# First unit of the mixer in four stages, a shorter way from routing to gather, and expert results merged during the last expert unit

## The chip, the cores and the metric

The kernel runs on one core of a Trainium2 chip. The metric is the device time of one execution in microseconds (us). TensorE (PE) multiplies, VectorE (DVE), ScalarE (ACT) and GpSimd (POOL) do the work between the products, and SyncE (SP) issues most of the DMAs. TensorE has two clock levels, 1.2 and 2.4 GHz.

## What is computed

A backbone of two layers over 256 context tokens and 256 latent tokens, 512 rows of 1024 numbers, all in float32. Each layer is

```python
hl = modulate(rmsnorm(xl, norm1[i]), sh1l, sc1l)       # the same for context, with its own shifts and scales
yc, yl = mixer(hc, hl, ...)                            # layer 0: RG-LRU and gated linear attention; layer 1: attention
xl = xl + g1l * yl
hl2 = modulate(rmsnorm(xl, norm2[i]), sh2l, sc2l)
xl = xl + g2l * hier_moe(hl2, ...)
```

The shifts, scales and gates (`sh`, `sc`, `g`, six rows of 1024 a layer and stream) are products of SiLU of a condition with `w_ada`, the adaLN columns. `hier_moe` takes for each token the best of four groups and in it the best two of four experts, and adds their results with their weights; an expert is `(silu(t @ w1) * (t @ w3)) @ w2`, 1024 to 512 to 1024. Layer 0 computes both streams, layer 1 only the latent one at its end.

## The kernel before

A float32 product is made of three: `whi` x `hhi`, `wlo` x `hhi` and `whi` x `hlo`, where `hi` is a value rounded by an ACT copy and `lo` the rest, a DVE (or POOL) subtraction of 128x1024. A weight tile `raw` is 1 MB (128 partitions x 2048); SP issues them in the order of a list (`plan`, `feed`, `pump`), one when a buffer (slot) comes free. The language's scheduler sets the order of each engine's instructions; each engine then works in that order.

**First unit.** `norm_T` loads the tokens into `xres`, squares them, turns them (transposes on PE into `acc` and `aux`) and scales them by the row factors into `xw`. `first_unit` computes the first 512 columns of the projection `w_in` as four sums (m) over eight blocks of 128 (k), in four steps n of two k each. Step n needs the adaLN columns n: `ad0` (8 matmuls `ad<-raw,cT`), and `ad0_cols`: an ACT copy, four transposes, and DVE's `v`, `A` and `B`. `finish` then applies `A` and `B` to `xw` and splits the result into `hhi` (ACT) and `hlo` (DVE). The list `AD0` says behind which product group each of the nine pieces is written. `LO_U0 = '1111'` puts the `wlo` of this unit on POOL. DVE also makes `lam`, a chain of small steps for the RG-LRU, at the same time.

**Route of layer 0.** After each tile's last products `route` makes logits and `choose` the ranks of groups and experts; the masks `Mb` go to PE, which counts per expert (`aux<-Mb,tri`). For tile 3 (`LATE_T`) the tokens' modulation (`xa`, `h2x`) runs on ACT and POOL. `route_end` with `units`, `weights`, `prepare` and `tables` ranks the experts by load: eight big ones get a unit of 128 rows each (a single unit), eight small ones share four units of 64 + 64 (two-expert units). One-hot matrices `oh` times `vals` give `t0i`, the rows that each unit gathers and scatters, and its weights `t0w`. POOL then clears `xg` and gathers the first two units' tokens from DRAM (`h2d`). The branch at line 1667, for overflow that doesn't occur with these inputs, follows. Copies `raw<-ident` on POOL hold back some weight DMAs.

**Experts of layer 0.** The loop `for e in range(NU)` goes over 12 units in the order `SEQ`; numbers 0 to 7 are single, 8 to 11 two-expert. In unit e `hidden(e, 1, 0)` and `(e, 1, 1)` make the product with w3, `he` multiplies it by the SiLU of the other, PE turns `he`, and ACT (and for a single unit DVE: `hl`) splits it; between these stand the first products of unit e + 1 (`hidden(e + 1, 0, 0)` and `(e + 1, 0, 1)`), then the product with w2. A two-expert unit isn't split; its matmuls are float32 on 64 columns, two records each. The result of unit e goes to DRAM (`yd`) by a scatter on POOL's queue, but for the last two (`N_LAST`), which stay as `yl` and are brought back to tokens by `back` matmuls. `get_parts` reads the scattered results back, two per token tile: `ya` and `yb` (for tiles 0 and 1 both halves of `pt`), in the order 2, 3, 0, 1, on POOL's queue; `add_parts` adds them on POOL, tile 0 on DVE. `finish_moe` adds `back`'s products, multiplies by the gate `row` and adds to `xres`; `norm1` and the `w_qkv` products of layer 1 follow. `LO_KV = "0101"` puts two `wlo` of `w_qkv` on POOL there.

Of the kernel before, what the change touches and what calls it, by code (L numbers as in the profile page):

```python
# [29 lines left out]
SEQ = (0, 8, 1, 2, 9, 3, 4, 10, 5, 6, 11, 7)  # L30
# [15 lines left out]
BEH = 3  # L46
FH = 1
# [11 lines left out]
TICK2 = 0  # L59
# [4 lines left out]
PIN = dict(pair='p', px='g', m0='p')  # L64
AT_SUM = 1
N_SP0 = 2
N_OH = 2
# [7 lines left out]
MID = 0  # L75
# [5 lines left out]
LO_KV = "0101"  # L81
# [9 lines left out]
BH = 1  # L91
AD0 = (1, 3, 3, 4, 5, 5, 8, 8, 8)
U0H = 1
Z_AT = (0, 0, 0, 0, 0, 4, 4, 0)
Z_Q = 0
LO_U0 = '1111'
# [6 lines left out]
AT = 3  # L103
LATE = 0
# [7 lines left out]
LATER = 0  # L112
CAP = 1
X_POOL = ()
F_ORDER = (2, 3, 0, 1)
P_DVE = (0,)
# [35 lines left out]
def backbone(ctx, tc, I, out):  # L152
# [229 lines left out]
    sp.dma_start(mod[0], I["bada"][0])  # L382
# [77 lines left out]
    def ad0_cols(n, sb, v, A1_0, B1_0, bn):  # L460

        act.activation(sb, ad0_ps.pop(n), AF.Copy)
        ps = aux()
        for c in range(4):
            pe.transpose(ps[:, c * P:(c + 1) * P], sb[:, c * P:(c + 1) * P], ident)
        dve.tensor_reduce(v, ps.rearrange("p (c g r) -> p c r g", c=4, g=4)[:, :, 0:2, :], axis=AX.X, op=ALU.add)
        v = v.rearrange("p (s k) i -> p s k i", s=2)
        ks = slice(2 * n, 2 * n + 2)
        nn, bb = (x.unsqueeze(2).to_broadcast([P, 2, 2]) for x in (n1c[:, 0, ks], b1c[:, 0, ks]))
        dve.tensor_tensor(A1_0[:, ks, :], v[:, 1], nn, op=ALU.mult)  # L470
        dve.tensor_tensor(B1_0[:, ks, :], v[:, 0], bb, op=ALU.add)
        dve.tensor_tensor(A1_0[:, ks, :], A1_0[:, ks, :], bn[:, ks, :], op=ALU.add)
# [102 lines left out]
    def unit_cols(name, b, hT, done, tokens_still, tiles=range(4), halves=(0, 1), after=None, on_act=True,  # L575
# [5 lines left out]
        if by_tile:  # L581
# [38 lines left out]
    def norm_T(hp, wide, bd):  # L620
# [3 lines left out]
        A1_0, B1_0, bn = (hp.tile([P, KD, 2], F32, name=n) for n in ("A1_0", "B1_0", "bn"))  # L624
        hhi = hp.tile([P, KD, NTOK], F32R, tag="hhi", name="hhi")
# [32 lines left out]
        for n in range(2):  # L658
            dve.scalar_tensor_tensor(bn[:, :, n:n + 1], b1c[:, 1, :].unsqueeze(2), 1.0, n1c[:, 0, :].unsqueeze(2),
                                     op0=ALU.add, op1=ALU.mult)  # L660

        def finish(n):

            if n == 0:
                scaled(6)
                scaled(7)
            ad0_cols(n, tmp("ad0"), hp.tile([P, 4, 2], F32, tag="v0", name="v0", bufs=2), A1_0, B1_0, bn)
            for k in (2 * n, 2 * n + 1):
# [5 lines left out]
                dve.tensor_tensor(hlo[:, k, :], xt, hhi[:, k, :].bitcast(F32), op=ALU.subtract)  # L674
            if n == 3:
                sp.dma_start(bd, I["bd"])
                sp.dma_start(mod[1], I["bada"][1])
        return (hhi, hlo), finish

    def first_unit(hT, finish, done):  # L680

        hh, hl = hT
        pss = [acc() for _ in range(4)]
        todo = [lambda n=n, f=f: f(n) for n in range(1, 4) for f in (lambda n: ad0(n, 0), lambda n: ad0(n, 1), finish)]
        at = list(AD0)
        ad0(0, 0)
        ad0(0, 1)
        finish(0)
        state["high"] = U0H
        for n in range(4):  # L690
            if n % 2 == 0:
                raw = feed(("w_in", 0, n // 2))
            state["lo"] = pool if LO_U0[n] == "1" else dve
            wh, wl = split(raw[:, n % 2 * 1024:(n % 2 + 1) * 1024])
            state["lo"] = dve
            for m in range(4):
                for kk in range(2):
                    w = [x[:, kk * 512 + m * P:kk * 512 + (m + 1) * P] for x in (wh, wl)]
                    k = 2 * n + kk
                    mm3(pss[m], w, (hh[:, k, :], hl[:, k, :]), k == 0, k == KD - 1)  # L700
                if n == 3:
                    done(m, pss[m])
                while at and at[0] == 4 * n + m:
                    at.pop(0)
                    todo.pop(0)()
        state["high"] = True
# [7 lines left out]
    tid = rt.tile([P, 4], F32, name="tid")  # L714

    def load_router():
# [7 lines left out]
                           base=0, channel_multiplier=-1)  # L724

# [72 lines left out]
    def route(l, NT, tmp, stream, h2_of, router):  # L798
# [12 lines left out]
        R.Mb = rt.tile([P, NT, NE], BF16, tag="Mb", name="Mb")  # L811

        def choose(t):
# [15 lines left out]
            dve.scalar_tensor_tensor(R.Mf[:, t], g0, 0.0, e01, op0=ALU.is_equal, op1=ALU.mult)  # L829
# [43 lines left out]
        def both(t):  # L873
            if MID and t == NT - 2 and not queue:

                queue.extend([lambda: None] * (MID - 1))
                queue.extend((lambda: turn(t, 1), lambda: logits(t, 1, 0), lambda: ends(t)))
                return
# [6 lines left out]
        def tile_(t, on_pool=False):  # L885
# [18 lines left out]
            hv = h2.rearrange("q (k p) -> q p k", k=KD)  # L904
            for n in range(2):
                a = tmp("xa2")
                if on_pool:
                    act.activation(a, x[:, n * 512:(n + 1) * 512], AF.Copy, scale=rss[t])
                    pool.tensor_tensor(a, a, A2[i][n], op=ALU.mult)
                else:  # L910
                    dve.scalar_tensor_tensor(a, x[:, n * 512:(n + 1) * 512], rss[t], A2[i][n], op0=ALU.mult, op1=ALU.mult)
                (pool if on_pool else dve).tensor_tensor(hv[:, n * 64:(n + 1) * 64, :], a.rearrange("q (p k) -> q p k", k=KD),
                    B2[i][n].rearrange("q (p k) -> q p k", k=KD), op=ALU.add)
            sp.dma_start(h2d[l][t * P:(t + 1) * P, :], h2)
# [5 lines left out]
    def route_end(R, l, NT, early=None):  # L920
# [16 lines left out]
        def weights():  # L937

            M = [st(f"M{k}", 4, 4) for k in range(2)]
            ek, tm = (rt.tile([P, 80], F32, tag=n, name=n)[:, 0:NT * NE].rearrange("p (t e) -> p t e", t=NT)  # L940
                      for n in ("ge", "gt"))
            g0 = R.rk[:, :, 0, :].unsqueeze(3).to_broadcast([P, NT, 4, 4])
            mk = [st(f"m{k}", 1) for k in range(2)]
            for k in range(2):
                for t in range(NT):
                    e_ = ek[:, t].rearrange("p (g e) -> p g e", g=4)
                    dve.tensor_scalar(e_, R.rk[:, t, 1:5, :], float(k), None, op0=ALU.is_equal)
                    dve.scalar_tensor_tensor(M[k][:, t], g0[:, t], 0.0, e_, op0=ALU.is_equal, op1=ALU.mult)
            M = [m.rearrange("p t g e -> p t (g e)") for m in M]
            for k in range(2):  # L950
# [1441 lines left out]
```

## Time and profile before

| | us |
|---|---|
| median of 3 runs (lowest, highest) | 1022.91 (1022.48, 1026.24) |
| profiled execution | 1020.54 |
| its span | 1018.8 |
| PE busy in it | 913.9 |
| DVE, ACT, POOL busy | 534.8, 396.2, 162.5 |

The span is the part of the execution between its first and last instruction. Times of rows are us from its start. A row of a timeline is an instruction or several of one form in a row (x3), with start, duration, and in brackets the idle time of the engine just ahead of it and what ended that. Durations of matmuls overlap: the next starts before the last has ended. Stages are cut here at 69 (end of the first unit), 298 (end of the mixer), 335 (first expert product), 565 and 617 (the last two units), 640, 790 and 1011.

### The profile page before, as it was taken

The page shows a single profiled execution, that of the slowest core. Times are in us where ns is not written, and L with a number is a line of the kernel's source. Part 1 is how long each engine was busy: PE and PEld are TensorE (multiplying, and loading weights), DVE is VectorE, ACT ScalarE, POOL GpSimd, SP SyncE. Part 2 cuts the span into 40 slices and gives each one's busy share as a digit, 9 for nine tenths or more (in the row PEclk, how much of TensorE's full clock was granted, in tenths as well). Part 3 has the DMA queues.
Part 4 walks back from the last instruction along what each step waited for, and adds up shares of the span by engine and source line. Part 5 has one row for each costly group of instructions (what it writes and reads, how often), then busy time and mean ns, then how long its engine had stood idle before and what let it go on. Part 6 is the DMA issues. An engine that isn't in the chain of part 4 may idle for free. (4 is left out here: it accounts for less than half of the span.)

```text
span 1018.8 us, 12604 instructions
## 1 busy us (share of the span) xinstructions
PE 913.9 (90%) x4549; PEld 535.3 (53%) x4549; DVE 534.8 (52%) x1039; ACT 396.2 (39%) x687; POOL 162.5 (16%) x163
## 2 busy tenths in 40 slices
PE   5899997999991899989999966998996899999997
PEld 3456465667761555647466433774575444443432
DVE  5458578538587565636456347878657111111112
ACT  3236745144231544637455423453545222121210
POOL 2103332040503400001100233023001000000000
PEclk9899999999995899999999978999998999999999
DMA  9925454559541899999999976845928699999993
GB/s 315 384 100 218 155 198 172 206 182 336 197 160 49 307 419 421 421 420 403 408 422 400 380 306 248 302 171 200 369 95 307 234 419 417 416 418 414 417 414 136
DMA packets 63165, 304.56 MB, mean 299 GB/s; under 512 B 8578, under 2 KB 17666, under 8 KB 35056
## 3 DMA queue, kind: packets, MB, share of 16 engines
q1 hardware_dynamic: 55216, 284.56, 71.4%
q0 software_dynamic: 5120, 14.06, 3.7%
q10 hardware_dynamic: 2752, 4.98, 1.3%
q8 instruction: 40, 0.66, 0.3%
q14 instruction: 37, 0.30, 0.1%
HBM read 294.76 MB, written 12.58 MB: 302 GB/s over the span
## 5 line engine op out<-in xcount | busy, mean ns | idle before, releaser
L144 DVE TENSOR_TENSOR wlo<-raw,whi 128x1024 fp32r<-128x1024 f32 x138 | 170.4, 1250 | 77.4 <-ACT whi L144 70.2
L144 ACT ACTIVATE whi<-raw 128x1024 fp32r<-128x1024 f32 x140 | 146.4, 1057 | 119.4 <-PE acc L144 100.4
L144 PE MATMUL aux<-raw,x 128*64 128x512 f32 x488 | 116.3, 597 | 2.0 <-PEq L2174 1.4
L144 PEld LDWEIGHTS aux<-raw,x 128*64 128x64 f32 x488 | 34.5, 136 | 62.9 <-issue 58.6
L144 PE MATMUL acc<-raw,xf 128*64 128x512 f32 x256 | 62.3, 598 | 2.2 <-DMA raw<-in_w_dram 2.2
L144 PE MATMUL aux<-raw,sl 128*64 128x512 f32 x240 | 58.7, 610 | 0.7 <-ACT sl L144 0.7
L144 PE MATMUL acc<-wlo,xh 128*128 128x512 f32 x128 | 52.1, 407 | 6.4 <-DVE wlo L144 3.6
L144 PE MATMUL ada<-raw,cT 128*32 128x512 f32 x320 | 54.7, 616 | 1.0 <-DMA raw<-in_w_ada_dram 1.0
L144 PE MATMUL acc<-whi,xh 128*128 128x512 f32 x128 | 53.5, 418 | 0.0
L144 PE MATMUL acc<-whi,xl 128*128 128x512 f32 x128 | 51.8, 405 | 0.0
L144 PE MATMUL acc<-raw,hf 128*64 128x512 f32 x128 | 38.6, 659 | 7.9 <-DMA raw<-in_w_dram 7.8
L144 DVE SCALAR_TENSOR_TENSOR aux<-aux,ws,mod 128x512 f32<-128x512 f32 x8 | 6.1, 760 | 73.3 <-PE aux L144 73.3
L144 PE MATMUL acc<-hhi,whi 128*128 128x512 f32 x96 | 38.5, 417 | 6.2 <-ACT hhi L144 6.2
L144 POOL DMA_INDIRECT yd<-y,t0i x10 | 11.7, 1173 | 191.6 <-ACT y L144 156.5
L144 PE MATMUL acc<-whi,h 128*128 128x512 f32 x128 | 41.7, 400 | 0.0
L144 PEld LDWEIGHTS acc<-raw,xf 128*64 128x64 f32 x256 | 19.1, 136 | 38.4 <-issue 30.9
L144 PE MATMUL acc<-hlo,whi 128*128 128x512 f32 x96 | 38.9, 406 | 0.2 <-DVE hlo L144 0.2
L144 PE MATMUL acc<-hhi,wlo 128*128 128x512 f32 x96 | 39.0, 406 | 0.0
L144 DVE TENSOR_TENSOR he<-sl,aux 128x512 f32<-128x512 f32 x8 | 8.4, 1056 | 56.2 <-PE aux L144 56.2
L144 PEld LDWEIGHTS aux<-raw,sl 128*64 128x64 f32 x240 | 18.2, 140 | 37.1 <-issue 35.0
L144 PEld LDWEIGHTS acc<-wlo,xh 128*128 128x128 f32 x128 | 25.1, 196 | 12.3 <-DVE wlo L144 4.0
L144 PEld LDWEIGHTS acc<-whi,xh 128*128 128x128 f32 x128 | 25.0, 195 | 10.1 <-issue 3.5
(444 smaller groups left out, 1850.5 us busy)
## 6 DMA issues: line engine op xcount, KB each, us to landing
raw<-in_w_dram SPq DMA_DIRECT2D x151, 1024.0 KB, 15.0
raw<-in_w_ada_dram SPq DMA_DIRECT2D x38, 1024.0 KB, 6.3
raw<-in_w_dram SPq DMA_DIRECT2D x72, 512.0 KB, 11.5
raw<-in_w_in_dram SPq DMA_DIRECT2D x10, 1024.0 KB, 5.1
raw<-in_w_ada_dram SPq DMA_DIRECT2D x32, 256.0 KB, 6.9
raw<-in_w_qkv_dram SPq DMA_DIRECT2D x6, 1024.0 KB, 12.8
xres<-in_w_dram SPq DMA_DIRECT2D x5, 1024.0 KB
raw<-in_w_out_dram SPq DMA_DIRECT2D x4, 1024.0 KB, 7.5
```

The costliest lines, as they stand in the source:

```text
L144: ins = f(*a, **k)
```

## The change

**First unit.** It is written as four stages. Products of step n come in groups of eight: `whi` x `hhi`, then the adaLN matmuls of n + 1, `whi` x `hlo`, the transposes of these columns, `wlo` x `hhi`. `wlo` is on DVE. The loads of `bada` (512 KB) go behind the unit, `pcol` and the `lam` chain ahead of the norm, `bn` to its start. What may run on which engine's early list (`PIN`) is changed with it.

**Route.** Tile 3's modulation is on DVE, half of its shift behind the choice. `choose` makes the masks `MM` per tile. `to_units` computes only the rows `ix`, with two one-hot steps of 128x512 and 8 matmuls, and the gathers follow at once; `experts` (the order of the weights), `others` (weights, count) and `weights_of` (8 more matmuls) come behind them, then the branch, then the first tokens' transposes and the first weight splits. The first two `xg` lie in one buffer that ACT clears. The copies `raw<-ident` are gone.

**Last units.** `SEQ` ends with 7, 11 in place of 11, 7, so that the last unit is a two-expert one. `get_parts` is written at the start of the last unit but one, `merge` in the last one: DVE adds `ya` and `yb`, multiplies by the gate and adds to `xres`, for tiles 2 and 3 ahead of the unit's second w3 half, for 0 and 1 ahead of its w2. `finish_moe` then only multiplies and adds. `LO_KV` is empty: all `wlo` of `w_qkv` are on DVE.

```diff
-SEQ = (0, 8, 1, 2, 9, 3, 4, 10, 5, 6, 11, 7)
+SEQ = (0, 8, 1, 2, 9, 3, 4, 10, 5, 6, 7, 11)
-PIN = dict(pair='p', px='g', m0='p')
+PIN = dict(pair='p', px='padg', re='da', tb='dag', m0='p', n1='pad', xa='pad')
-LO_KV = "0101"
+LO_KV = ""
-LO_U0 = '1111'
...
     def first_unit(...)
+        for n in range(3):
+            products(n, 0, w)
+            for h in range(2):
+                ad0(n + 1, h)
+            copy, turn, rest = columns(n + 1)
+            copy()
+            x, hi = weights_hi(n + 1)
+            products(n, 1, w)
+            turn()
+            rest()
+            products(n, 2, w)
+            modulate(n + 1)
+            w = hi, weights_lo(x, hi)
+        sp.dma_start(bd, I["bd"])
+        for l in range(2):
+            sp.dma_start(mod[l], I["bada"][l])
...
-    R.finish()
+    R.finish(lambda R: [f() for f in late_h2])
...
-    R.prepare(True)
-    slot_of = R.pk, R.vals
-    ix, wgt = R.tables(0, "t0")
+    ix, weights_of, slot_of = R.to_units()
...
+    for e in range(2):
+        fetch_x(e)
+    R.experts()
...
+    R.others()
+    wgt = weights_of()
...
+    def merge(t):
+        ya, yb = parts[t]
+        dve.tensor_tensor(ya, ya, yb, op=ALU.add)
+        for n in range(2):
+            sl = slice(n * 512, (n + 1) * 512)
+            dve.tensor_tensor(ya[:, sl], ya[:, sl], g2[int(t < 2)][n], op=ALU.mult)
+        dve.tensor_tensor(xres[:, t, :], xres[:, t, :], ya, op=ALU.add)
...
+        if e == NU - N_LAST:
+            get_parts()
...
         hidden(e, 1, 0)
-        get_parts(0, e)
+        if e == NU - 1:
+            for t in F_ORDER[:2]:
+                merge(t)
         hidden(e, 1, 1)
...
+        if e == NU - 1:
+            for t in F_ORDER[2:]:
+                merge(t)
         py = [acc(), acc()]
...
-            y = parts[t][0][:, sl]
-            dve.tensor_tensor(y, ps, y, op=ALU.add)
-            dve.tensor_tensor(y, y, g2[int(t < 2)][n], op=ALU.mult)
-            (pool if (t, n) in X_POOL else dve).tensor_tensor(xres[:, t, sl], xres[:, t, sl], y, op=ALU.add)
+            y = parts[t][1][:, sl]
+            dve.tensor_tensor(y, ps, g2[int(t < 2)][n], op=ALU.mult)
+            dve.tensor_tensor(xres[:, t, sl], xres[:, t, sl], y, op=ALU.add)
```

PE's instructions in the first unit, from the transposes of the first adaLN columns on (`ad`), first before, then after; `hhi`, `hlo` are the tokens, `raw,cT` the adaLN matmuls:

```order
L144 MATMUL aux<-ident,ad_307 128x128 x4
L144 MATMUL ad_343<-raw,cT 32x512 x3
L144 MATMUL acc<-hhi,whi 128x512 x3
L144 MATMUL ad_343<-raw,cT 32x512
L144 MATMUL acc<-hlo,whi 128x512
L144 MATMUL acc<-hhi,wlo 128x512
L144 MATMUL acc<-hhi,whi 128x512
L144 MATMUL acc<-hlo,whi 128x512
L144 MATMUL acc<-hhi,wlo 128x512
L144 MATMUL acc<-hlo,whi 128x512
L144 MATMUL acc<-hhi,wlo 128x512
L144 MATMUL acc<-hhi,whi 128x512
```

```order
L131 MATMUL aux<-ident,ad_301 128x128 x4
L131 MATMUL acc<-hhi,whi 128x512 x8
L131 MATMUL ad_340<-raw,cT 32x512 x8
L131 MATMUL acc<-hlo,whi 128x512 x8
L131 MATMUL aux<-ident,ad_349 128x128 x4
L131 MATMUL acc<-hhi,wlo 128x512 x8
L131 MATMUL acc<-hhi,whi 128x512 x8
L131 MATMUL ad_397<-raw,cT 32x512 x8
L131 MATMUL acc<-hlo,whi 128x512 x8
L131 MATMUL aux<-ident,ad_411 128x128 x4
L131 MATMUL acc<-hhi,wlo 128x512 x8
L131 MATMUL acc<-hhi,whi 128x512 x8
```

The adaLN matmuls of the next step stand together behind the first eight products, and the three kinds of product are no longer mixed one by one.

POOL's instructions from the last row factor (`r`) to the gathers (`xg<-h2d`), before and after; `xa` and `h2x` are the modulation of tile 3:

```order
L144 TENSOR_TENSOR r_2365<-ssq,half_neg 128x1
L144 COPY raw<-ident 128x1
L144 TENSOR_TENSOR xa_2424<-xa_2424,row 128x512
L144 TENSOR_TENSOR h2x<-xa_2424,row 128x64x8
L144 TENSOR_TENSOR xa_2428<-xa_2428,row 128x512
L144 TENSOR_TENSOR h2x<-xa_2428,row 128x64x8
L144 MEMSET xg 128x1024
L144 COPY raw<-ident 128x1
L144 DMA xg<-h2d_112,t0i 128x1024
L144 MEMSET xg 128x1024
L144 DMA xg<-h2d_112,t0i 128x1024
```

```order
L131 TENSOR_TENSOR r_2305<-ssq,half_neg 128x1
L131 TENSOR_TENSOR r_2386<-ssq,half_neg 128x1
L131 DMA xg_2528<-h2d_113,ix 128x1024 x2
L1776 TENSOR_LOAD cnti
L1777 COMPARE_AND_BRANCH
```

Between the last row factor and the gathers nothing is left on POOL.

DVE's instructions at the end of the experts. Before, from the tokens of the last unit (`xl`) to its `hl`; after, from the `he` of the last unit but one over its `hl` to the merge of the third tile (`pt`):

```order
L144 TENSOR_TENSOR xl<-aux,xh 128x512 x2
L144 TENSOR_TENSOR wlo<-raw,whi 128x1024 x2
L144 TENSOR_TENSOR he<-sl,acc 128x128x4
L144 TENSOR_TENSOR wlo<-raw,whi 128x1024 x2
L144 TENSOR_TENSOR pt<-pt 128x1024
L144 TENSOR_TENSOR wlo<-raw,whi 128x1024 x2
L144 SCALAR_TENSOR_TENSOR yl<-acc,t0w,yl 128x512 x2
L144 TENSOR_TENSOR wlo<-raw,whi 128x1024 x3
L144 TENSOR_TENSOR he<-sl,acc 128x128x4
L144 TENSOR_TENSOR wlo<-raw,whi 128x1024
L144 TENSOR_TENSOR hl<-aux,hh 128x512
```

```order
L131 TENSOR_TENSOR he<-sl,acc 128x128x4
L131 TENSOR_TENSOR wlo<-raw,whi 128x1024 x2
L131 TENSOR_TENSOR ya<-ya,yb 128x1024
L131 TENSOR_TENSOR ya<-ya,row 128x512 x2
L131 TENSOR_TENSOR xres<-xres,ya 128x1024
L131 TENSOR_TENSOR ya<-ya,yb 128x1024
L131 TENSOR_TENSOR ya<-ya,row 128x512
L131 TENSOR_TENSOR hl<-aux,hh 128x512
L131 TENSOR_TENSOR ya<-ya,row 128x512
L131 TENSOR_TENSOR pt<-pt 128x1024
L131 TENSOR_TENSOR xres<-xres,ya 128x1024
L131 TENSOR_TENSOR pt<-pt,row 128x512 x2
```

One addition of parts stood among the splits before; now one merge and a half stand ahead of `hl`, and the rest of the four, with the two `yl` of that unit, ahead of the last unit's `he`.

## Rows read from the trace of the kernel before

**Rows 1.** Windows: us, busy PE, PEld, DVE, ACT, POOL, PEclk, DMA share, GB/s.
```profile
0.00:69.00 69.00, 52.57 (x218) 29.20 (x219) 31.88 (x86) 21.12 (x34) 12.12 (x16) 0.95 0.82 285
69.00:298.00 229.00, 219.27 (x1313) 144.51 (x1312) 160.03 (x268) 102.40 (x171) 64.35 (x62) 0.99 0.54 197
298.00:335.00 37.00, 12.79 (x99) 8.34 (x97) 25.25 (x110) 8.34 (x14) 11.61 (x14) 0.61 0.32 111
335.00:565.00 230.00, 220.96 (x974) 136.77 (x972) 128.09 (x142) 126.20 (x155) 27.35 (x26) 0.98 0.99 403
565.00:617.00 52.00, 42.98 (x158) 21.66 (x157) 17.89 (x17) 13.81 (x17) 13.52 (x12) 0.90 0.89 354
617.00:640.00 23.00, 12.21 (x52) 7.02 (x51) 21.62 (x41) 10.50 (x23) 8.76 (x4) 0.71 0.55 212
...
790.00:1011.00 221.00, 216.70 (x1036) 90.86 (x1036) 35.92 (x78) 39.49 (x75) 0.00 (x0) 0.98 0.92 373
```

**Rows 2.** Timeline of PE, first unit: start, us, instruction, idle before and its end.
```profile
27.03 1.65 PE L144 MATMUL acc<-hhi,whi 128*128 128x512 f32 x3 [4.34 <-ACT hhi L144]
...
32.33 0.63 PE L144 MATMUL acc<-hhi,wlo 128*128 128x512 f32 x1
...
36.61 1.06 PE L144 MATMUL ad<-raw,cT 128*32 128x512 f32 x8
...
68.75 0.39 PE L144 MATMUL acc<-hlo,whi 128*128 128x512 f32 x1
68.97 0.39 PE L144 MATMUL acc<-hhi,wlo 128*128 128x512 f32 x1
```

**Rows 3.** Timelines of DVE and POOL, first unit.
```profile
14.14 0.17 DVE L144 TENSOR_SCALAR lam<-lam 128x8 f32<-128x8 f32 x1
...
20.49 4.65 POOL L144 TENSOR_TENSOR wlo<-raw,whi 128x1024 fp32r<-128x1024 f32 x2 [7.30 <-ACT whi L144]
20.60 2.27 DVE L144 TENSOR_SCALAR lam<-lam 128x8 f32<-128x8 f32 x1
...
22.91 2.26 DVE L144 TENSOR_TENSOR lam<-lam,lam 128x8 f32<-128x8 f32 x1
```

**Rows 4.** Timelines of POOL, DVE and PE, route of layer 0.
```profile
306.38 1.32 POOL L144 TENSOR_TENSOR h2x<-xa,row 128x512 f32<-128x512 f32 x1
306.49 1.31 DVE L144 TENSOR_TENSOR gt<-lg 128x80 f32<-128x80 f32 x1
...
316.19 1.22 DVE L144 TENSOR_TENSOR wlo<-raw,whi 128x1024 fp32r<-128x1024 f32 x1
...
323.57 3.70 PE L144 MATMUL aux<-vals,oh 128*128 128x36 f32 x14 [1.12 <-DVE vals L144]
...
328.79 1.25 POOL L144 DMA_INDIRECT xg<-h2d,t0i  x1 [8.31 <-DVE t0i L144]
...
335.16 0.79 PE L144 MATMUL acc<-whi,xh 128*128 128x512 f32 x1
...
343.50 0.70 PE L144 MATMUL acc<-wlo,xh 128*128 128x512 f32 x1 [2.77 <-PEq L1667]
```

**Rows 5.** Timelines of PE, POOL and DVE, last two expert units of layer 0.
```profile
565.22 4.50 PE L144 MATMUL acc<-raw,xf 128*64 128x512 f32 x18
...
576.56 0.60 POOL L144 DMA_DIRECT2D ya<-yd  x1 [7.95 <-DMA yd<-y,t0i]
...
596.00 2.39 POOL L144 TENSOR_TENSOR ya<-ya,yb 128x1024 f32<-128x1024 f32 x1 [4.87 <-DMA yb<-yd]
...
598.83 1.23 DVE L144 TENSOR_TENSOR pt<-pt 128x1024 f32<-128x1024 f32 x1 [19.87 <-DMA pt<-yd]
...
601.24 0.79 PE L144 MATMUL acc<-wlo,xh 128*128 128x512 f32 x1 [3.61 <-DVE wlo L144]
```

**Rows 6.** Timelines of PE and DVE, from the last expert product to layer 1.
```profile
617.18 1.09 PE L144 MATMUL acc<-yl,back 128*128 128x512 f32 x4
...
620.18 1.28 DVE L144 TENSOR_TENSOR pt<-pt,row 128x512 f32<-128x512 f32 x2
...
637.41 2.18 PE L144 MATMUL aux<-ident,pt 128*128 128x128 f32 x9 [4.76 <-DVE pt L144]
```

More of the change, by code (lines that the diff above doesn't have):

```diff
@@ L657, in norm_T, with columns, modulate @@
             scaled(k)
[L658 to L667, printed above, removed]
+        def columns(n):
+            sb, v = tmp("ad0"), hp.tile([P, 4, 2], F32, tag="v0", name="v0", bufs=2)
+            return (lambda: act.activation(sb, ad0_ps.pop(n), AF.Copy),
+                    *ad0_cols(n, sb, v, A1_0, B1_0, bn))
+        def modulate(n):
             for k in (2 * n, 2 * n + 1):
@@ L673, in finish @@
                 act.activation(hhi[:, k, :], xt, AF.Copy)
[L674 to L680, printed above, removed]
+            for k in (2 * n, 2 * n + 1):
+                dve.tensor_tensor(hlo[:, k, :], xts[k], hhi[:, k, :].bitcast(F32), op=ALU.subtract)
+        for t in range(4):
+            turn(6, t)
@@ L682, in first_unit, with turn_last, weights_hi, weights_lo @@
+        def turn_last():
+            for t in range(4):
+                turn(7, t)
+        return (hhi, hlo), (columns, modulate, scaled, turn_last)
+    def first_unit(hT, parts, done):
         hh, hl = hT
+        columns, modulate, scaled, turn_last = parts
         pss = [acc() for _ in range(4)]
-        todo = [lambda n=n, f=f: f(n) for n in range(1, 4) for f in (lambda n: ad0(n, 0), lambda n: ad0(n, 1), finish)]
-        at = list(AD0)
+        raws = {}
+        def weights_hi(n):
+            if n % 2 == 0:
+                raws[n // 2] = feed(("w_in", 0, n // 2))
+            x, y = raws[n // 2][:, n % 2 * 1024:(n % 2 + 1) * 1024], split_p.tile([P, 1024], F32R, tag="hi", name="whi")
+            act.activation(y, x, AF.Copy)
+            return x, y
+        def weights_lo(x, hi):
+            y = split_p.tile([P, 1024], F32R, tag="lo", name="wlo")
+            dve.tensor_tensor(y, x, hi.bitcast(F32), op=ALU.subtract)
+            return y
+        def product(n, m, kk, j, w):
+            k = 2 * n + kk
+            a, b = ((w[0], hh), (w[0], hl), (w[1], hh))[j]
+            pe.matmul(pss[m], a[:, kk * 512 + m * P:kk * 512 + (m + 1) * P], b[:, k, :],
+                      start=(k == 0 and j == 0), stop=(k == KD - 1 and j == 2))
+        def products(n, j, w):
+            for m in range(4):
+                for kk in range(2):
+                    product(n, m, kk, j, w)
@@ L686, in first_unit @@
         ad0(0, 0)
         ad0(0, 1)
[L688 to L705, printed above, removed]
@@ L709, in backbone @@
+        sp.dma_start(bd, I["bd"])
+        for l in range(2):
+            sp.dma_start(mod[l], I["bada"][l])
+        for m in range(4):
+            for kk in range(2):
+                for j in range(3):
+                    product(3, m, kk, j, w)
+            done(m, pss[m])
     rwt = rt.tile([P, 2, KD, 20], F32, name="rwt")
@@ L873, in both @@
         def both(t):
[L874 to L877 removed]
+            if l == 0 and t == NT - 2 and not queue:
+                queue.extend((lambda: None, lambda: turn(t, 1), lambda: logits(t, 1, 0), lambda: ends(t)))
                 return
@@ L1015, in prepare @@
+        def prepare(room=None):
+            tp_ = rt.tile([P, NT, NE], F32, tag="tm", name="tp_")
+            R.pk = [st(f"pk{k}", 1) for k in range(2)]
             R.vals = []
+            if room is None:
+                vals = rt.tile([P, 2, NT, 3, NE], F32, tag="vals", name="vals")
+                room = lambda n: vals[:, int(n[-1])]
             at = pos
@@ L1673, in backbone @@
                 spare(0, wk, d4, e, jx, jw, 1)
+    pin("px")
+    prep_x(0)
+    pin("tb")
+    ahead()
+    pin("px")
+    prep_x(1)
+    more_slots(parts_p, N_PARTS)
     pin("m0")
-    if LO0:
-        state["lo"] = pool
     hidden(0, 0, 0)
-    state["behind"] = None
     hidden(0, 0, 1)
-    if LO0 < 2:
-        state["lo"] = dve
+    for f in state["hold"]:
+        f()
+    state["hold"] = None
     parts = {}
```

345 lines of the change are left out of this document (192 added, 153 removed).

## The prediction

> **What bounds the kernel now.** I read the stages first [rows 1]. TensorE is busy 219 of 229 us in the mixer (69 to 298), 221 of 230 in the first experts (335 to 565), 217 of 221 in the last ones (790 to 1011). The holes are the start (53 of 69), the route of layer 0 (13 of 37), the end of its experts (43 of 52) and the seam to layer 1 (12 of 23), and the change works on exactly these four. From 335 to 565 the DMA engines are 0.99 busy at 403 GB/s too, so a gain of PE alone is kept there only as far as the weight stream comes earlier with it. In the mixer (0.54) and the attention layer the DMA has room, and from 790 on PE waits for next to nothing, so what is gained upstream reaches the end. Then, in each hole, the timeline shows what PE waits for.
>
> **Part A, the first unit (0 to 69).** The first product stands at 27.03, after 4.34 us without one, and waits for `hhi` [rows 2]. Ahead of it two tiny `lam` steps of DVE took 2.27 and 2.26 us, just while POOL subtracts `wlo` [rows 3]; the others of their kind take 0.17. The change gives those `wlo` to DVE and the `lam` steps to the time before the norm: 27.03 less 4.2, less some 0.6 for `bn` and the steps moved ahead, is 22.2. Products start 0.23 us apart [rows 2], so 24 of one n are 5.5 us; one set of adaLN columns is 8 matmuls, which the profile records as 16, at 1.06 for 8, so 2.1; four transposes 0.3: 7.9 us a stage. Before, the first products ran at the half clock (1.2 GHz) to past 32.33, where one still takes 0.63 instead of 0.39 [rows 2]; 5.7 us at half speed cost 2.8, and I leave that in. So n=1 starts at 33, n=2 at 41, n=3 at 49, and the 96th product at 49 + 5.5 + 1 (one adaLN row) = 55.5. Before, the 96th product stands at 68.97, and the other work done by then is the same. That is 13.5. Each stage must have its `hhi` in time (columns, copy, transposes, DVE, ACT, some 5 us in a row, beside 16 products of 3.7 us), and may stand late by a little; three waits of 0.5 leave **12**. Ends: 15 if the clock stays full, 7 if three waits and the adaLN tiles cost 2 each. The moved `wlo` are 1.22 each [rows 4] on a DVE that is busy 32 of 69. What is late next is unit 1's weights; with the DMA 0.82 busy to 69 there is room to bring them some 12 earlier, so I charge nothing.
>
> **Part B, the route (298 to 335).** On POOL four products of tile 3 (1.3 each) stretch DVE's choice, as `gt` at 306.49 with 1.31 beside `h2x` at 306.38 [rows 4]. On DVE the counts come 1.3 earlier without them. Behind them three `wlo` (1.22) leave the chain for 3.7; the one-hot matrices are made four at a time and the 8 matmuls, 3.70 for 14 records spread over waits, run together, for 2.5; order and weights, about 1, go behind the gather. Sum 8.5: the gather is issued at about 320.3, not 328.79. But what is moved behind it now stands ahead of the transposes: 8 more matmuls (to 328.5) and the branch, which held PE 2.77 at 343.50; then ACT and DVE make the first splits, which were hidden before. Transposes at 331.5 to 333, first product at 335.1, which is where it is now (335.16). What is gained on PE is the later stall, 2.77, and the half clock behind it, less that of the new wait: 3.5. The eight copies that hold back weight DMAs go, and the stream restarts about 7 earlier. Since both limits lie together in this stage, I take **4.5**, from 1 (the branch costs 6) to 8 (all of the stream).
>
> **Parts C and D, end of the experts (565 to 640).** The work from 565.22 on is the same on PE: the last units are swapped. The first of them is now single; its 24 products (5.5) stand for 32 records of 0.25 (8.2) [rows 5], so this point comes at 562.5, counted without A and B. Nothing is gained on the fetch: it waits for the scatter of the unit before, until 576.56, 11.3 after this point, which makes 573.8. The second tile's `yb` allowed POOL's add at 596.00, 19.4 after the fetch.
>
> The cost lies on DVE. All merges stand ahead of the last `he`, and one and a half of them ahead of `hl` of the single unit, without which PE has no third product of its w2. PE is there at 562.5 + 5.5 + 8.2 + 0.8 = 577. At the old pace `hl` is ready at 573.8 + 19.4 + 1.23 + 0.65 + 0.65 = 595.7, and PE waits 19 us; such a wait is seen now, DVE's 19.87 for `pt`, but only `wlo` stood behind it, and PE lost 3.61 [rows 5]. Then w2 5.5 and 2.5 more at half clock, w3 8, `he`, transposes and copy 2.4, w2 8 and four returns 1: 623, against 617.18 now: 6 later. At best the four parts (2.1 MB) come alone at 403 GB/s, 5.2 us: `hl` at 581.6, end at 608, 9 sooner. The real transfer is nearer to the slow row, since as many weights are still out; B lets the stream lead by some 3.5 more: end at 619.4, **2 later**.
>
> The Trainium skill ("DMA: Bandwidth & Descriptors", section "Queues, rings and completion order") says that each DMA engine takes turns between the queues that have work. By that rule the parts get half of the traffic, and the sum is 5.5 smaller, as rival (1) works it out; the row of 596.00, 19.4 us after the fetch, speaks against even turns.
>
> Behind the end, `finish_moe` has two DVE steps a half instead of four, 8 of 0.64 less over two tiles, 5.1 [rows 6]; the two `wlo` of `w_qkv` leave POOL, beside which tiny steps of DVE are stretched there as in [rows 3], and cost DVE 1.2 each. Now the second tile's transposes stand at 637.41, 20.2 after 617.18; I take 7.5 less, from 4 to 9. C and D: 2 - 7.5 = **-5.3**, ends -15 and +2.
>
> **Sum.** 12 + 4.5 + 5.3 = 21.8. The profiled execution took 1020.54, which leaves 998.7; the median of the runs lies 2.4 above it, so **1001**.
>
> **Rivals.** (1) Parts and weights share the traffic evenly: 2.1 MB at half of 403 GB/s take 10.4 us, `hl` is there at 586.8, 5.5 before my value (592.3), 995.5. For it: the parts have a queue of their own beside SP's; against: 19.4 us, with nearly the same weights out. 0.14. (2) The route gives PE nothing: the branch stands in front of the first splits and takes 6; the stream then restarts when it did, 1005.5. For it: every engine has to pass it, and now with nothing left to do; against: the array stood only 2.77. 0.12. (3) The first unit is no pipeline: PE takes the adaLN matmuls in their place, and waits for their weight tiles there, n=3 at 55: A is 6, 1007. For it: the DMA is full up to 51; against: the order of the feeds is the order of use. 0.11. With (2) and (3) and the parts at the old pace together the time is 1015 or more, within 0.5% of before: 0.07. (4) Slower: `hl` of the single unit waits on the merges, one us of end for one us of wait. To come out over 1028 the second pair must land 46 us after its fetch, not 16 to 19, as if fetch and weights stood in one line and the attention weights went first. Nothing of that is seen; a kernel that fetches and merges in this order has only this place where one wait has no bound from PE. 0.05. My forecast, with the smaller spread of its own, holds 0.51.
>
> **How the numbers follow.** 988 takes the good ends of A and C together, 1013 the bad ends of A and B with the old pace of the parts; some 0.1 lies on either side. A measurement of this kernel tells about 0.5%, 5 us, from no change. Faster by more needs under 1017.8: all cases but the last two, 0.88. Same: 0.07. Slower: 0.05.
>
> **What would show it.** In the new profile: the 96th product near 55 to 57, and no DVE step of over 2 us beside POOL; the first gather near 308 to 309 (320 less 12), the first expert's product some 12 earlier than 335.16 and no stall behind it; in the last two units a PE wait of about 15 us for DVE's `hl`, with `ya` waiting for DMA ahead of it, and half clock behind; the seam to layer 1 some 13 us instead of 20. If the wait for `hl` is under 5 us, C is larger by 10; if the 96th product is past 62, A has failed; if PE waits for weights from 790 on, gains were not carried.

## The result, and the profile after

The changed kernel takes **1010.14 us** (median, 1008.28 to 1010.72), beside 1023.49 for the kernel before, measured with it (1022.48 to 1026.24): ratio **0.986**, 95% interval 0.984 to 0.989. The forecast was 1001, with a range of 988 to 1013: the direction and the range held, but of the 21.8 us forecast only some 13 came. The profiled execution took 1008.28, its span 1006.6 (1018.8 before).

First the stages, the view of [rows 1] cut at the same places of the program: us, busy time and instructions of PE, PEld, DVE, ACT, POOL, then granted clock, DMA share and GB/s. The cut at 551.30 lies 13.7 before 565, as the matmuls do that were done by then.

```profile
0.00:57.40 57.40, 45.06 (x224) 28.00 (x225) 33.21 (x94) 22.04 (x34) 2.69 (x12) 0.97 0.99 349
57.40:288.00 230.60, 220.23 (x1316) 144.60 (x1315) 159.78 (x273) 102.55 (x170) 62.41 (x62) 0.99 0.53 194
288.00:325.00 37.00, 16.52 (x114) 12.89 (x112) 21.38 (x89) 7.30 (x11) 5.65 (x7) 0.63 0.43 152
325.00:551.30 226.30, 218.25 (x969) 138.90 (x968) 137.07 (x150) 132.59 (x162) 25.95 (x22) 1.00 0.98 398
551.30:610.00 58.70, 37.05 (x151) 17.01 (x149) 24.75 (x27) 7.98 (x11) 5.78 (x9) 0.83 0.80 319
610.00:626.00 16.00, 10.79 (x42) 5.74 (x44) 14.65 (x33) 9.54 (x20) 1.49 (x2) 0.88 0.69 249
626.00:779.50 153.50, 139.59 (x717) 96.03 (x711) 109.87 (x302) 73.75 (x205) 26.38 (x29) 0.96 0.67 248
779.50:1000.40 220.90, 216.43 (x1038) 91.42 (x1039) 37.07 (x76) 40.79 (x76) 0.00 (x0) 0.99 0.92 372
```

The first unit is 11.6 shorter (57.4 for 69), the seam to layer 1 is 7 (16 for 23). The last two units are 6.7 longer (58.7 for 52), with PE busy 37 us instead of 43: a wait has come in there. And one stage in which the forecast saw no cost, the attention layer, is 3.5 longer (153.5 for 150).

**First unit.** The timelines of PE and DVE (start, us, instruction, idle before and its end), for [rows 2, 3]:

```profile
22.52 2.54 PE L131 MATMUL acc<-hhi,whi 128*128 128x512 f32 x8 [2.11 <-ACT hhi L131]
24.99 1.92 PE L131 MATMUL ad<-raw,cT 128*32 128x512 f32 x16
...
31.52 2.54 PE L131 MATMUL acc<-hhi,whi 128*128 128x512 f32 x8 [0.24 <-ACT hhi L131]
40.53 2.54 PE L131 MATMUL acc<-hhi,whi 128*128 128x512 f32 x8 [0.25 <-ACT hhi L131]
...
57.36 0.39 PE L131 MATMUL acc<-hhi,wlo 128*128 128x512 f32 x1
```
```profile
20.75 0.15 DVE L131 TENSOR_TENSOR B<-v,b1c 128x4 f32<-128x4 f32 x1
```

The pipeline runs as drawn: eight products, sixteen records of adaLN, and a wait of a quarter of a us ahead of each stage from the second on. The 96th product stands at 57.36 (68.97 before), and no small DVE step is stretched.

**Route.** PE ahead of the first expert's product, POOL's gather, and then the windows of the weight stream, 16 us each and 10 earlier in after than in before, whose row comes first:

```profile
310.29 1.25 POOL L131 DMA_INDIRECT xg<-h2d,ix  x1 [18.70 <-DVE aux L131]
```
```profile
321.74 3.61 PE L131 MATMUL aux<-ident,xg 128*128 128x128 f32 x16 [4.15 <-DVEq L1777]
325.31 0.50 PE L131 MATMUL acc<-whi,xh 128*128 128x512 f32 x1
```
```profile
332.00:348.00 16.00, 11.85 (x45) 9.47 (x46) 6.24 (x6) 7.50 (x9) 3.44 (x7) 0.75 0.73 264
```
```profile
322.00:338.00 16.00, 15.24 (x66) 11.92 (x66) 11.99 (x12) 14.23 (x18) 8.23 (x8) 0.90 0.69 242
```

The gather is issued at 310.29, 18.5 earlier than in [rows 4], of which 10.1 come from the mixer. The branch (line 1777 now) stands ahead of the transposes, and the first expert product is 9.85 earlier than 335.16, so the route itself gave PE nothing up to there. What it gave lies behind: PE is busy 15.24 of 16 us instead of 11.85, with the stall of 2.77 gone. But the stream brings no more than before in the same stretch, 242 GB/s for 264.

**Last two units and seam.** The fetch on POOL's queue, the merges on DVE, and PE:

```profile
561.46 0.60 POOL L131 DMA_DIRECT2D ya<-yd  x1 [8.22 <-DMA yd<-y,ix]
```
```profile
573.43 1.23 DVE L131 TENSOR_TENSOR ya<-ya,yb 128x1024 f32<-128x1024 f32 x1 [15.40 <-issue]
...
580.80 1.23 DVE L131 TENSOR_TENSOR ya<-ya,yb 128x1024 f32<-128x1024 f32 x1 [3.56 <-DMA yb<-yd]
...
582.67 0.68 DVE L131 TENSOR_TENSOR hl<-aux,hh 128x512 fp32r<-128x512 f32 x1
```
```profile
583.41 0.80 PE L131 MATMUL acc<-whi,hl 128*128 128x512 f32 x1 [20.50 <-DVE hl L131]
584.01 0.63 PE L131 MATMUL acc<-whi,hh 128*128 128x512 f32 x1
...
610.08 1.21 PE L131 MATMUL acc<-yl,back 128*128 128x512 f32 x4
...
620.68 0.33 PE L131 MATMUL aux<-ident,pt 128*128 128x128 f32 x1 [3.29 <-DVE pt L131]
622.93 2.61 PE L131 MATMUL aux<-ident,pt 128*128 128x128 f32 x11 [1.93 <-DVE pt L131]
```

`hl`, a step of 0.68 us, stands in DVE's row behind a merge whose `yb` lands 19.3 after the fetch, and PE waits **20.50** for it; behind that it runs at the lower clock (0.63 a product) for ten products. The last w2 ends 7.1 earlier than at 617.18, the second tile's transposes stand 14.5 earlier than at 637.41 [rows 6].

By these rows the shift of the same work is, in us: first unit -11.6; mixer +1.5; route and experts -2.3 (the fetch is 15.1 earlier than 576.56, of which the swap of the units makes 2.7 and the stages ahead 10.1); last two units **+5.3**; seam -7.4; from there to the route of layer 1 **+4.1**; and the end -1.8. The sum is -12.2, as the spans say.

Each of these shifts compares one trace with one, and traces differ. The kernels of experiments 1, 2, 7 and 8 below have the same instructions as the whole change on every engine up to the first expert product, that of experiment 3 up to the branch; experiment 6 has those of the kernel before up to the seam. The latest 96th product of the former (experiment 3), and that of experiment 6:

```profile
58.91 0.39 PE L131 MATMUL acc<-hhi,wlo 128*128 128x512 f32 x1
```
```profile
71.46 0.39 PE L144 MATMUL acc<-hhi,wlo 128*128 128x512 f32 x1
```

These stand beside 57.36 and 68.97, and the first expert product of experiments 1, 2, 7 and 8 lies between 326.67 and 328.90, beside 325.31. So 1.5 to 3.6 us up to there are spread between traces of the same instructions, and the trace of the whole change is the earliest of its kind. The mixer's +1.5 and the -2.3 of route and experts are not clear of this spread.

### The profile page after: what moved, and what is told of

The parts are those of the page before. It is cut to its first block, busy times and chain, and to the rows that moved or that the text cites. A ratio compares the mean times of both kernels' runs of the same rounds, so it can differ in the third digit from the quotient of the medians.

```text
span 1006.6 us, 12582 instructions
## 1 busy us (share of the span) xinstructions
PE 905.5 (90%) x4565; PEld 535.6 (53%) x4565; DVE 540.6 (54%) x1040; ACT 396.5 (39%) x686; POOL 130.3 (13%) x142
## 5 line engine op out<-in xcount | busy, mean ns | idle before, releaser
L131 DVE TENSOR_TENSOR wlo<-raw,whi 128x1024 fp32r<-128x1024 f32 x144 | 174.3, 1231 | 64.7 <-ACT whi L131 62.4
L131 PE MATMUL acc<-whi,hl 128*128 128x512 f32 x64 | 26.4, 413 | 20.5 <-DVE hl L131 20.5
L131 PEld LDWEIGHTS acc<-raw,xf 128*64 128x64 f32 x256 | 19.2, 136 | 38.6 <-issue 30.0
L131 PE MATMUL acc<-raw,hf 128*64 128x512 f32 x128 | 34.5, 600 | 4.3 <-DMA raw<-in_w_dram 4.3
L131 POOL DMA_INDIRECT yd<-y,ix x10 | 11.9, 1192 | 198.5 <-ACT y L131 182.2
L131 PE MATMUL acc<-hlo,whi 128*128 128x512 f32 x96 | 35.9, 409 | 0.0
L131 PE MATMUL acc<-hhi,wlo 128*128 128x512 f32 x96 | 35.0, 400 | 0.0
L131 ACT ACTIVATE x<-gat,B,A 128x256 f32<-128x256 f32 x26 | 13.3, 561 | 41.6 <-PE gat L131 40.8
```

Source lines behind the costliest of these rows:

```text
L131: ins = f(*a, **k)
```

## The experiments

**1. Merges behind the last `he`.** The changed kernel, with DVE held to the written order from the single unit on (`dve.on`), tiles 0 and 1 merged behind the last unit's `he`, tiles 2 and 3 behind `norm1` of the others.

```diff
-F_ORDER = (2, 3, 0, 1)
+F_ORDER = (0, 1, 2, 3)
...
+        if e == NU - 2:
+            dve.on = True
...
-        if e == NU - 1:
-            for t in F_ORDER[:2]:
-                merge(t)
...
-            for t in F_ORDER[2:]:
+            for t in F_ORDER[:2]:
                 merge(t)
...
+    dve.on = True
+    for t in F_ORDER[2:]:
+        merge(t)
+    dve.on = False
     finish_moe(2)
```

> The changed kernel with the merges moved: DVE works in the written order in the last two units; the merges of tiles 0 and 1 (whose parts are fetched first) stand behind the last unit's he, those of tiles 2 and 3 behind the finish of tiles 0 and 1. Theory (PE stands 20.5 us for hl, behind merges that wait for the parts): the wait goes, the w2 products of the single unit follow at once, and the last unit is held by its own work and its weights alone: end of w2 of the last unit 15 to 20 us earlier (about 591 to 595 instead of 610), seam 0 to 5 us longer; total 995 to 1002, 9 to 14 under the changed kernel. Rival (the weight stream of the two-expert unit is the real limit there, and the wait for hl only hides it): PE then waits for weight tiles instead, total 1006 to 1010.

Measured: 998.28 us (997.44 to 1001.53), ratio 0.976 (0.972 to 0.980). DVE and PE of its trace:

```profile
562.92 0.69 DVE L131 TENSOR_TENSOR hl<-aux,hh 128x512 fp32r<-128x512 f32 x1 [1.38 <-ACT hh L131]
...
585.77 1.23 DVE L131 TENSOR_TENSOR pt<-pt 128x1024 f32<-128x1024 f32 x1 [2.39 <-DMA pt<-yd]
```
```profile
592.22 1.21 PE L131 MATMUL acc<-yl,back 128*128 128x512 f32 x4
...
629.26 0.87 PE L131 MATMUL aux<-ident,xn 128*128 128x128 f32 x3 [6.48 <-DVE xn L131]
```

The parts still land some 21 after the fetch, but the merges now wait for them where nothing stands behind. `hl` comes at once, and the last w2 ends at 592.2 instead of 610.1. Some of that is given back: DVE makes the merges of tiles 2 and 3 when PE already wants their `xn`, and PE waits 6.48. So the merges ahead of `hl` cost the whole change 8 to 10 us (by the ratios of this run and of its repetition, number 7), as the theory said.

**2. The old end.** The changed kernel with units, fetch, adds and `finish_moe` as before, but all `wlo` of `w_qkv` on DVE.

```diff
-SEQ = (0, 8, 1, 2, 9, 3, 4, 10, 5, 6, 7, 11)
+SEQ = (0, 8, 1, 2, 9, 3, 4, 10, 5, 6, 11, 7)
...
-            y = parts[t][1][:, sl]
-            dve.tensor_tensor(y, ps, g2[int(t < 2)][n], op=ALU.mult)
+            y = parts[t][0][:, sl]
+            dve.tensor_tensor(y, ps, y, op=ALU.add)
+            dve.tensor_tensor(y, y, g2[int(t < 2)][n], op=ALU.mult)
```

> The changed kernel with the end of the experts undone: order 11, 7, parts added on POOL (tile 0 on DVE), the long finish, as in the kernel before; all wlo of w_qkv stay on DVE. Theory (the merges cost in the units what they bring in the seam, and the fillers that stood in the old stalls have to be done later): the end of the experts as before, shifted by 12.6; total 1007 to 1011, within 3 us of the changed kernel. Rival (the new tail is a gain of 5 or more, as forecast): 1015 or more.

Measured: 1009.62 (1007.17 to 1011.80), ratio 0.987 (0.982 to 0.991), no different from the whole change, as the theory said. The new end, as the change orders it, nets nothing: the +5.3 of the last units eats the some 3 that the shorter `finish_moe` brings. The seam takes 16.1 here (from the last w2 at 606.92 to the second tile's transposes at 622.98), 12.9 in the whole change and 20.2 before.

**3. Without the branch.** The changed kernel without the layer-0 test for overflow and the path behind it, which these inputs don't take; this leaves that part of the kernel out.

```diff
-    rv = nc.values_load(R.cnt[0:1, 0:1], min_val=0, max_val=NTOK)
-    with tc.If(rv > 0):
...
-                spare(0, wk, d4, e, jx, jw, 1)
```

> The changed kernel without the branch of layer 0 to the spare path for overflow: the test of the count and the spare path are left out, and the path isn't taken with these inputs. Theory (the branch now stands ahead of the first splits; slots come free only behind it, so the weight stream restarts late and the DMA-bound experts keep only a part of the shorter route): first splits 3 to 5 us earlier, the stream and the experts 2 to 4 earlier, total 1006 to 1008. Rival (the stream is held by something else, such as the gathers, or the stage is held by PE): PE's first product 3 to 4 earlier, the stage ends as now, total 1009.5 to 1010.5.

Measured: 1009.77 (1008.04 to 1011.92), ratio 0.987 (0.983 to 0.991). The medians don't tell it from the whole change; the time lies in the range of the rival. In the trace, the wait of 4.15 ahead of the transposes becomes this:

```profile
319.73 1.95 PE L131 MATMUL aux<-ident,xg 128*128 128x128 f32 x8
323.40 1.94 PE L131 MATMUL aux<-ident,xg 128*128 128x128 f32 x8 [1.73 <-DMA xg<-h2d,ix]
```

The second gather ends the wait now, and PE, 1.5 later than in the whole change before the route, is 0.3 earlier at the first expert product (324.99). The branch costs PE some 2 us there, not the 6 of rival (2); the expectation had 3 to 5 for the first splits, and DVE's are 2.0 earlier (323.29 for 325.29). Whether those 2 reach the end the times can't say.

**4. The new first unit with `wlo` on POOL, and 5. the old one with `wlo` on DVE.** Between them and the two kernels stands a square: order old or new, engine POOL or DVE.

```diff
# 4, in the changed kernel, weights_lo
-            dve.tensor_tensor(y, x, hi.bitcast(F32), op=ALU.subtract)
+            pool.tensor_tensor(y, x, hi.bitcast(F32), op=ALU.subtract)
# 5, in the kernel before
-LO_U0 = '1111'
+LO_U0 = '0000'
```

> The changed kernel with the four wlo of the first unit on POOL again, in its new order. Theory (of the 11 us gained up to the end of the first unit about 4 come from taking these subtractions away from POOL, beside which small DVE steps wait, and the rest from the order): the 96th product 3 to 5 us later than 57.4, total 1013 to 1015. Rival (it is the order alone, since the lam steps now stand ahead of the norm and nothing small is left beside POOL): 96th product within 1 us, total 1010 to 1011.

> The kernel before, with one thing changed: the four `wlo` of the first unit are made on DVE instead of POOL, in the old order of the first unit. With the kernels before and after and the run of the new order with `wlo` on POOL this makes a square of two by two. Theory (POOL beside DVE's small steps is the cost, and the order matters only once it is gone): the two `lam` steps shrink from 2.27 to 0.2, so the first product comes 4 us earlier, at 23; the old order still lets PE wait for each column set, so the 96th product stands between 61 and 65 (68.97 before, 57.36 after), and the median is 4 to 8 us under before, 1015 to 1019. Rival 1 (the engine is everything): 96th product at 58 to 59, median 1012 to 1013. Rival 2 (in the old order nothing hangs on the engine, since DVE gets 4.9 us more to do ahead of the products): 96th product at 67 to 69, median 1021 to 1023.

Measured: number 4 took 1020.99 (1018.26 to 1023.28), ratio 0.997 (0.995 to 0.999); number 5 1015.21 (1013.33 to 1017.18), ratio 0.992 (0.990 to 0.995). DVE, POOL and PE of number 4, then PE of number 5:

```profile
21.87 2.33 DVE L131 TENSOR_TENSOR B<-v,b1c 128x4 f32<-128x4 f32 x1
...
34.35 1.41 DVE L131 TENSOR_TENSOR A<-v,n1c 128x4 f32<-128x4 f32 x1
```
```profile
21.84 2.34 POOL L131 TENSOR_TENSOR wlo<-raw,whi 128x1024 fp32r<-128x1024 f32 x1 [8.35 <-ACT whi L131]
33.36 2.38 POOL L131 TENSOR_TENSOR wlo<-raw,whi 128x1024 fp32r<-128x1024 f32 x1 [9.18 <-ACT whi L131]
```
```profile
25.76 0.49 PE L131 MATMUL acc<-hhi,whi 128*128 128x512 f32 x1 [4.23 <-ACT hhi L131]
...
37.44 0.49 PE L131 MATMUL acc<-hhi,whi 128*128 128x512 f32 x1 [1.48 <-ACT hhi L131]
...
67.43 0.39 PE L131 MATMUL acc<-hhi,wlo 128*128 128x512 f32 x1
```
```profile
59.69 0.39 PE L144 MATMUL acc<-hhi,wlo 128*128 128x512 f32 x1
```

The 96th product stands at 68.97 (old order, POOL), 67.43 (new, POOL), 59.69 (old, DVE) and 57.36 (new, DVE). Moving four subtractions gives 9.3 alone and 10.1 in the new order; the order gives 1.5 alone and 2.3 with the move, no more than traces of the same instructions differ by. So the engine's part is shown, and a gain of the order by itself is not. In the pipeline each `wlo` on POOL meets a step of the chain that makes the next `hhi`, and PE waits 1.48 where it waited 0.24. Of the 10.1 the stretched steps are 5.9 (2.2 in the first stage, some 1.25 in each of the other three). 0.9 lies ahead of them, where the norm starts later in this trace; in the last stage DVE has two `wlo` of the next unit (2.35) in the chain as well, and PE waits 2.79; and the first eight products run at the lower clock level (0.56 from 25.76 to 29.66, 1.4 longer than in the whole change). The time follows: the median of number 4 is 10.9 over that of the whole change. All expectations of number 4 were too low. In number 5 the 96th product is nearest to the rival that the engine is everything, and the time, 7 below before, to the good end of the theory. That is less than the 9.3, and its trace shows where some was lost: in the mixer PE stands 1.28 at 246.55 and 0.58 at 249.35 for DVE, and then runs at the lower clock level, as this window of 4 us shows (0.57).

```profile
252.00:256.00 4.00, 4.00 (x13) 3.13 (x12) 1.44 (x1) 1.06 (x1) 3.22 (x4) 0.57 0.01 3
```

The +1.5 of the changed kernel in its mixer comes in smaller steps spread over the stage, and none of the runs settles its cause.

**6. `wlo` of `w_qkv` on DVE alone.**

```diff
-LO_KV = "0101"
+LO_KV = ""
```

> The kernel before, with one thing changed: the two `wlo` of `w_qkv` that POOL makes at the seam to layer 1 are made on DVE. Theory (of the 7.4 us that the seam got shorter in the changed kernel, 5.1 are the eight DVE steps fewer per pair of tiles, and the rest comes from POOL being still): the second tile's transposes come 2 us earlier than 637.41, the median is 1020 to 1022. Rival (DVE pays for the two `wlo` what it gains on its small steps): the transposes stay within 0.7 us of 637.41, the median within 1 us of before.

Measured: 1020.15 (1019.46 to 1023.01), ratio 0.998 (0.997 to 1.000). Its trace is 1.7 late ahead of the seam (the last w2 ends at 618.86), with the same instructions. The second tile's transposes stand here, 2.45 before 637.41:

```profile
634.96 2.18 PE L144 MATMUL aux<-ident,pt 128*128 128x128 f32 x9 [0.60 <-DVE pt L144]
```

So this edit alone shortens the seam by some 4.2, more than expected, and of the 7.4 of the whole change only some 3 are left for the shorter `finish_moe`. But from there to the first gather product in the route of layer 1 it loses 3.6. Its span is 1.1 shorter than before, its median 2.3.

**7 and 8. Experiment 1 again, and with more fillers.** Three adaLN steps instead of one behind `finish_moe` of tiles 2 and 3, for the wait of 6.48 for `xn`.

```diff
-KA = 1
+KA = 3
```

> The changed kernel with the merges behind the last `he` once more, beside its next version in the same comparison: 996 to 1001, as in its first run (998.28).

> The changed kernel with the merges behind the last `he` (as in the run of that), and with three instead of one of the adaLN steps of layer 1 behind `finish_moe` of tiles 2 and 3, where PE waited 6.5 us for DVE's `xn`. Theory (the 18 adaLN matmuls that the changed kernel shows in the full attention stage cost their own time there, and nothing in a wait): 48 records of 0.12 us move out of it into that wait; 4 to 6 us less than the version with one step, 993 to 995, with the wait for `xn` at 0 to 2 us. Rival (the weights of these steps, 1 MB each, come at the cost of those of w_qkv and attention, or are not there in time): the wait for DVE turns into one for DMA, 997 to 1002.

Measured: 999.97 (999.17 to 1003.17), ratio 0.979 (0.977 to 0.981), and 997.88 (995.33 to 1000.04), ratio 0.976 (0.974 to 0.978). The edit did not do what it says. In the trace 32 adaLN records stand between the first `pt` and the first `xn` transpose in both, since the scheduler puts them where it has room, and in the second only 8 of them in the gap:

```profile
622.25 1.06 PE L131 MATMUL ada<-raw,cT 128*32 128x512 f32 x8
627.81 0.87 PE L131 MATMUL aux<-ident,xn 128*128 128x128 f32 x3 [4.50 <-DVE xn L131]
```

The 2.1 between the medians were there before the last units (2.5 by the traces), in stages that the edit does not touch, and lie within the spread of such traces; so it says nothing on fillers in that wait. Both versions beat both kernels.

## Why the prediction was right, and where it was off

**Part A held, partly by luck**: 12 forecast, 11.6 measured, the 96th product at 57.36 for "55 to 57". The first product came at 22.52 for 22.2, and the pipeline works as written. But the 2.8 of half clock that the sum kept did not come (the granted clock is 1.00 from 22.5 to 43), while a stage took 9.0 where I had 7.9 and a wait of 0.5, and the last part 7.8 where I had 6.5; these errors cancel. What the sum did not see is how much hung on the engine: it charged POOL's place with 4.2 of the 13.5 and the interleaving with the rest, and the square shows some 9 to 10 for the engine. The two stretched `lam` rows [rows 3] were only the part of it that was easy to see; the kernel before has another, in the chain to the third step:

```profile
47.21 2.44 DVE L144 TENSOR_TENSOR B<-v,b1c 128x4 f32<-128x4 f32 x1
```

The Trainium skill ("SBUF — State Buffer", section "Who interferes with whom") says that a DVE instruction with two SBUF inputs contends with a GpSimd instruction that reads SBUF; the rows of experiment 4 agree, with 0.15 turning into 2.33 for `B` beside a `wlo` of 2.34. The mixer then gave 1.5 back, which the sum did not have; that is within the spread of the traces.

**Part B was half right**: forecast 4.5, measured 2.3. The route itself was counted well: gather at 310.29 for "308 to 309", with 8.4 gained on it for 8.5, first product 9.85 earlier, the stall of 2.77 and the half clock behind it gone. The step that failed is "the stream restarts about 7 earlier". One `raw` is issued early, at 311.58. The next stands behind the branch in SP's own queue, at 322.09, which is as far behind the mixer as the first one of before (332.51, less 10.1). Those after it (327.68, 335.71) wait for slots, which come free as DVE's `wlo` of the first expert use them up; these start at 325.29, while the kernel before had made three of them inside the route (316.19 to 320.44). So the fourth tile is no earlier than before (345.40, less 10.1). The view of waits of SP's queue from 311 to 345 (us in total, times, longest), for the whole change and for experiment 3:

```profile
SPq L131 <- DVE wlo L131: 15.9, 3, 7.5
SPq L1777 <- SPq L1777: 6.4, 1, 6.4
```
```profile
SPq L131 <- DVE wlo L131: 22.7, 3, 10.3
```

Without the branch the second tile is issued at 314.79, but the queue only waits longer for the slots, and the third and fourth are 2.0 and 0.5 earlier (325.67, 335.24). Hence 242 GB/s in 16 us for 264 at the same distance from the mixer. The gain that PE keeps behind the first product is 2.5 up to the fetch (236.15 us for 241.40, less the 2.7 of the swap), about the old stall and no more, as [rows 1] made likely with a DMA share of 0.99. Rival (2) had this half right, and the price of the branch wrong.

**Part C failed in its size**: +2.2 forecast (619.4 for 617.18), +5.3 measured. The mechanism was the one written down: `hl` behind the merges, half clock behind it. One of its terms was mis-sized: I let the parts come 3.5 faster than at the old pace, "B lets the stream lead", while they took 19.3 against 19.4 before. The fetch also came at 561.46 instead of 573.8 - 16.5 = 557.3, but that is what A, B and the mixer did not bring, and it is counted there. Together that is 7.6, and `hl` was ready that much after my 592.3 - 16.5. My slow row, 623 and "6 later", was the right one. Rival (4)'s exchange of one us of end for one us of wait held: with `hl` 7.6 later than my value, the end came 7.2 later (610.08 for 619.4 - 16.5). Its far point was never near; by its own sum (15.9 and 27 more) it is 43 us behind the fetch, not 46.

The time of rival (1), the parts there after 10.4 us, did not come; they took 19.3. Its idea of turns is not refuted, and the trace says why. The queues of DMA from the fetch to the landing of the second tile's `yb` in the changed kernel, 561.5 to 580.8 (packets, MB, share):

```profile
q1 hardware_dynamic: 703, 5.05, 62.6%
q0 software_dynamic: 818, 3.01, 38.7%
```

Two things were wrong in the rival's sum. The queue of the parts (q0) got 37% of the bytes (3.01 of 8.07 MB) and not half. And it moved 3.01 MB in that time, not 2.1, since the parts of the other two tiles, fetched right behind, lie in the same queue. The profile counts nearly as many packets for the weights (q1, 7.2 KB each) as for the parts (3.7 KB each). The rule that I cited in the prediction from the Trainium skill ("DMA: Bandwidth & Descriptors", section "Queues, rings and completion order") has the turns go by packets. Even turns of packets of these two sizes would give the parts 34% of the bytes, by my estimate, where I had read half; the trace is near it over the whole wait, but not in each part of it (0.97 of 4.24 MB, 23%, from 562 to 572, and 2.53 of 4.12 MB from 572 to 582). Whether the packets of the profile are the rule's no run shows.

**Part D held**: 7.5 forecast, 7.4 measured, but its split did not. POOL's two `wlo` made 4.2, for which I had 2.4, and the eight DVE steps some 3, for which I had 5.1. The 4.2 are two tiny steps that DVE made beside these `wlo` in the kernel before, and that take 0.15 and 0.16 in experiment 6:

```profile
629.84 2.33 DVE L144 TENSOR_TENSOR rs_t<-r 128x1 f32<-128x1 f32 x1
632.70 2.12 DVE L144 SCALAR_TENSOR_TENSOR rs_t<-rs_t,ssq 128x1 f32<-128x1 f32 x1
```

**A term was missing**: behind the seam 4.1 are given back. 1.4 of it go up to the first `xn` transpose, and 2.7 from there to the first gather product of layer 1. The experiments place most of it. This is that gather product in the kernel before, in experiments 6 and 2, and in the whole change:

```profile
790.27 0.58 PE L144 MATMUL acc<-oh,h2hi 128*128 128x256 f32 x1 [0.78 <-DVE oh L144]
```
```profile
791.41 0.58 PE L144 MATMUL acc<-oh,h2hi 128*128 128x256 f32 x1 [0.78 <-DVE oh L144]
```
```profile
779.26 0.58 PE L131 MATMUL acc<-oh,h2hi 128*128 128x256 f32 x1 [0.81 <-DVE oh L131]
```
```profile
779.91 0.58 PE L131 MATMUL acc<-oh,h2hi 128*128 128x256 f32 x1 [2.52 <-DVE oh L131]
```

From the second tile's transposes (637.41, 634.96, 622.98, 622.93) that is 152.9 before and 153.7 in experiment 5, which both keep `LO_KV`; 156.5 and 156.3 in experiments 6 and 2, which empty it and keep the old end; 157.0 in the whole change. So some 3 of the 4.1 come with the two `wlo` of `w_qkv` on DVE, the same edit that gains 4.2 in the seam, and only about 1 of its gain is kept. How it costs them is open; PE waits for such a `wlo` only 0.64 (experiment 6) and 1.34 (experiment 2). That adaLN fillers had no stall left to lie in, as the expectation of experiment 2 has it, does not explain it: in that stretch experiments 6 and 2 have 104 adaLN records, as many as the kernel before. The assumption behind the sum was that what is gained ahead of the attention layer is kept through it, because DMA has room there; that was not enough.

Point by point the errors are 0.4 (A), 1.5 (mixer), 2.2 (B), 3.1 (C), 0.1 (D) and 4.1 (behind the seam), and 1.8 the other way at the end, 9.6 in all (21.8 forecast, 12.2 by the spans); nearly all against the forecast, since each stage's gain was counted as kept unless a row spoke against it.

## What to carry to other kernels

Before a merge or an add that waits for a DMA is put on an engine, look at what stands behind it in that engine's row: here a step of 0.68 us stood behind a transfer of 19.3, and moving the merges behind it gave another 8 to 10 us over the whole change. Try the engine of an operation apart from its order: four subtractions moved from POOL to DVE were worth 9 to 10 us up to the end of the first unit, the reordering 1.5 to 2.3, which is no more than two traces of the same instructions differ by. Follow a gain to the end: of the 4.2 that two more of these moves brought in the seam, some 3 were lost behind it. And where two limits lie together, as PE and the weight stream do in the experts, a gain of one is worth only what the other brings with it: count the slots that let it go on, not the time of the first issue.

## What the runs showed of the hardware

Small DVE steps of 128x4 take 0.15 alone and 1.41 to 2.33 beside POOL's subtraction of 128x1024 (experiment 4), steps of 128x1 2.12 and 2.33 (the seam of the kernel before), and it is the steps in the chain to the next product that were hit, in experiment 4 once in each stage. Transfers on POOL's queue, next to weights on SP's, got 3.01 of 8.07 MB in 19.3 us, with packets of half the size, and their first two pairs took 19.2 to 19.4 in the kernel before, the whole change and experiment 2, whichever unit ran beside them. In experiment 5 two waits of PE, 1.28 and 0.58 at 246.55 and 249.35, were followed by products at the lower clock level (0.57 over 4 us).
